# Layer 0's modulation steps ordered on TensorE behind the block traced before them

## The chip, the cores and the metric

The kernel runs on one core of one Trainium2 chip. The metric is the time of one execution in device microseconds (us), from the runtime's measurement; a profiled execution also leaves a trace, whose span runs from the first to the last instruction. Lower is better. Differences below about 0.2% are not told apart from none.

## The reference, cut to what matters

Two transformer-like layers are applied to 128 context tokens and 256 latent tokens (384 rows of 1024 features). Layer 0 mixes with two groups of linear recurrences (HGRN2 and gated DeltaNet), layer 1 with attention; each layer ends with an MLP. Every sub-layer is modulated by vectors that come from a conditioning vector and one matrix, `ada_w`, of 1024 x 6144 per layer:

```python
def _modulation(cond, w, b):
    m = jax.nn.silu(cond) @ w + b
    return jnp.split(m[:, None, :], 6, axis=-1)
...
        p_sh1, p_sc1, p_g1, p_sh2, p_sc2, p_g2 = _modulation(c_ctx[None, :], ada_w[l], ada_b[l])
        s_sh1, s_sc1, s_g1, s_sh2, s_sc2, s_g2 = _modulation(c, ada_w[l], ada_b[l])
        hp = _rmsnorm(xp, norm_g[l, 0]) * (1.0 + p_sc1) + p_sh1
...
        q_a, f_fw, f_bw, i_a, g_a, qkv_b, g_b, a_fw, a_bw, b_fw, b_bw = _split(h @ w_in, _AB_SIZES)
...
        xp = xp + p_g1 * mp
        hp = _rmsnorm(xp, norm_g[l, 1]) * (1.0 + p_sc2) + p_sh2
```

What the change moves is the part of layer 0's modulation that the mixer does not need at its start: the gate of the mixer (`g1`, columns 2048 to 3071 of `ada_w`), and the shift and scale of the MLP's norm (`sh2`, `sc2`, columns 3072 to 5119).

## The kernel before, in words

Everything is computed in float32 precision by pairs of reduced-precision products: each weight tile is loaded by the SP queue into a ring `raw`, split into a high part by ACT (L209) and a low part by DVE or POOL (L210), and multiplied on PE in three products (high by high, high by low, low by high).

The framework builds the queue of each engine ahead of time: it plays the program through a model of the chip and, whenever an engine is free, gives it the ready instruction that was traced earliest. The order thus made is fixed; on the chip each engine works through its own queue in that order, and waits where data are late. A context `issue_after` adds order edges to that planning: what is traced inside it on the engine of a given instruction is put in that engine's queue behind that instruction. It adds no instruction and no semaphore. The table `ORDER` (L40 to L49) and the method `behind` (L141) apply it: `self.mark` remembers an instruction under a name, and a block traced under a key of `ORDER` is queued behind the marks listed there.

Layer 0 is the function `layer0` (L1411). After a first part that ends with `gdn_solve` being traced (a triangular solve of 31 steps on POOL, L1052 and L1053), a hand-written list `STEPS` (L55) interleaves three generators with the blocks of the input projection:

- `h`, the HGRN2 chain (`hgrn_steps`, `hgrn_rest`): elementwise work on DVE (L746 to L783) between small products on PE (L745, L757, L762, L831 to L848);
- `d`, the DeltaNet chain (`gdn_steps`): products at L1086 to L1192;
- `a`, the modulation (`ada_rest`, L372);
- blocks `f`, `q`, `c` and `g` by `fm_block` (L633), each of 48 products at L645 to L647, and blocks `v` by `tm_half` (L677), each of 72 products at L687 to L689. In the list they stand in the order f3, f1, f2, q1, q0, c4, c5, v0, v1, c0, c1, g0, g1, g2, g3.

The modulation has twelve loading steps. Eight come from `ada_quad` (L313; here called S0 to S7): each loads two tiles of 512 KB (L323) and makes four products into one PSUM bank (L326), which the trace holds as eight records. Four come from `ada_half` (L353; H0 to H3), with loads at L362 and products at L367. All loads go through a ring `adr` of two slots, and one step fills both: the loads of a step can only start when the products of the step before have freed the slots. After S7 and after H3 the sums are copied to SBUF by DVE (L383 and L384, or L394), spread to columns by four small products into a bank called `tmp` (L488), and added to the bias (L490).

In `STEPS` the twelve steps are traced like this: S0 and S1 after q1; S2 and S3 after q0; S4 after q0 as well, ahead of c4; S5 after c4; S6 and S7 with the first spread after c5; H0 after v1; H1, H2, H3 with the second spread at the very end, after g3. The planner is free to queue them elsewhere.

Behind the list come `mix_out(1, t)` (L1255, through the same `tmp` bank), the output projection (`tm_parts`, products at L672 to L674), the residual and the norm of the MLP, which needs the result of H3, and the MLP.

Of the kernel before, what the change touches and what calls it, by code (L numbers as in the profile page):

```python
# [19 lines left out]
KT = 8  # L20
# [28 lines left out]
}  # L49

PARTS = [range(0, 2), range(2, 4), range(4, 6), range(6, 8)]
# [55 lines left out]
class Trunk:  # L107
# [525 lines left out]
    def fm_block(self, src, hh, evac, key):  # L633

        nc = self.nc
        hhi, hlo = hh
        raw = self.slab(src.rearrange("(k p) n -> p k n", p=P), KT, 256)
        whi, wlo = self.split_w(raw, KT, 256, pool=ON_POOL.get(key, ()))
        pg = [self.ps([P, T], "acc") for _ in range(2)]
        for g in range(2):  # L640
            with self.behind(key, g):
                for n in range(2):
                    c = slice(n * P, (n + 1) * P)
                    for k in range(g * 4, g * 4 + 4):
                        nc.tensor.matmul(pg[n], whi(k)[:, c], hhi[:, k], start=(k == 0), stop=False)  # L645
                        nc.tensor.matmul(pg[n], whi(k)[:, c], hlo[:, k], start=False, stop=False)  # L646
                        nc.tensor.matmul(pg[n], wlo(k)[:, c], hhi[:, k], start=False, stop=(k == KT - 1))  # L647
        for n in range(2):
            evac(n, pg[n])

# [26 lines left out]
    def tm_half(self, src, hh, evac):  # L677

        nc = self.nc
        hhi, hlo = hh  # L680
        whi, wlo = self.split_w(self.slab(src.rearrange("(k p) n -> p k n", p=P), KT, 256), KT, 256)
        for t0, n in ((0, 2), (2, 1)):
            pg = self.ps([P, 2, 256], "acc")[:, 0:n]
            for t in range(t0, t0 + n):
                c = slice(t * P, (t + 1) * P)
                for k in range(KT):
                    nc.tensor.matmul(pg[:, t - t0], hhi[:, k, c], whi(k), start=(k == 0), stop=False)  # L687
                    nc.tensor.matmul(pg[:, t - t0], hlo[:, k, c], whi(k), start=False, stop=False)
                    nc.tensor.matmul(pg[:, t - t0], hhi[:, k, c], wlo(k), start=False, stop=(k == KT - 1))  # L689
            evac(t0, n, pg)  # L690
            yield

# [718 lines left out]
    def layer0(self):  # L1411
        nc, i = self.nc, self.i
# [47 lines left out]
        def gate(b):  # L1460
            o = (2048, 2304, 4096, 4352)[b]
            self.fm_block(W[:, o:o + 256], hh, lambda n, pg: self.evac_gate(b * 2 + n)(pg), f"gate{b}")

        def value(b):
            for _ in self.tm_half(W[:, 1536 + b * 256:1792 + b * 256], hh, lambda t, n, pg: nc.scalar.activation(
                    self.va[:, t:t + n, b * 256:b * 256 + 256], pg, AF.Copy)):
                pass

        def hgrn():
            yield from self.hgrn_steps()  # L1470
            yield from self.hgrn_rest()

        chains = {"h": hgrn(), "d": self.gdn_steps(), "a": self.ada_steps}
        for step in STEPS.split():
            kind, n = step[0], int(step[1:] or 1)
            if kind in chains:
                for _ in range(n):
                    next(chains[kind], None)
            elif kind == "f":
                self.fm_block(fcol(n // 2, n % 2), hh, fgate(n // 2, n % 2), step)  # L1480
            elif kind == "q":
                self.fm_block(W[:, n * 256:n * 256 + 256], hh, lambda k, pg: self.evac_q(n * 2 + k)(pg), step)
            elif kind == "c":
                self.fm_block(qkv(n), hh, conv(n), step)
            elif kind == "v":
                value(n)
            elif kind == "g":
                gate(n)
            elif kind == "m":
                y = [self.sb([P, 4, T], "hyB", F32R) for _ in range(3)] + [self.m12([P, 4, T], F32R)]  # L1490
                yy = Halves(y[0::2]), Halves(y[1::2])
                for t in range(NT):
                    self.mix_out(0, t, yy, "hg")
# [6 lines left out]
        step = self.proj_residual(i["w_out_ab"][0], yy, scr, (("wo", "wo"), ("wo", "m12")), order,  # L1500
                                  lambda t: self.mix_out(1, t, yy, "tmp"))
# [10 lines left out]
        step = self.mlp(0, hh, order=order)  # L1512
# [308 lines left out]
```

## Time and profile before

| | |
|---|---|
| median of 3 runs | 1133.59 us (1132.84 to 1134.93) |
| the profiled execution | 1139.19 us |
| its span | 1137.3 us |
| PE busy | 1081.7 us |
| DVE busy | 762.3 us |
| POOL busy | 277.2 us |

Times in views count from the start of the span. A row of the timeline has the start, the length, the engine, the line, the operation, the tile written and those read, the shape and the count of merged instructions; idle time of the engine ahead of it stands in brackets with what ended it. Rows of DMA-issuing instructions (SPq) give the time of the issue, not of the transfer. In a table of windows each engine has its busy time and its number of instructions, then follow the granted clock of PE (1.00 is full), the busy share of the DMA engines and their rate.

### The profile page before, as it was taken

What the parts mean: (1) busy time and instruction counts of PE and PEld (TensorE: products, weight loads), DVE (VectorE), ACT (ScalarE), POOL (GpSimd) and SP (SyncE); (2) the same over time, 40 slices, a digit from 0 to 9 for tenths busy, and PEclk for the clock granted to TensorE, in tenths of its full rate; (3) what the DMA queues carried; (4) which work ended last, traced back from release to release, by engine and by line L of the source; (5) the groups of instructions that cost most, each with busy time, mean ns of one, the idle gap of its engine ahead of it and who ended that gap; (6) DMA issues with size and microseconds to landing.
All of it is one profiled execution on the core that took longest, in us unless ns stands there. A gap on an engine that the chain in (4) does not pass through costs nothing.

```text
span 1137.3 us, 17975 instructions
## 1 busy us (share of the span) xinstructions
PE 1081.7 (95%) x6853; PEld 937.8 (82%) x6853; DVE 762.3 (67%) x1188; ACT 485.1 (43%) x874; POOL 277.2 (24%) x295
## 2 busy tenths in 40 slices
PE   6989969999998999999999999999988999999998
PEld 3868857988986898888889788888668889998987
DVE  3678499995467698968887654878748773333333
ACT  4464333342445543433334444656636433333330
POOL 0054894231204011111112252324012011111102
PEclk9989989999998999999999999999989999999999
DMA  8953725333162687766674147566425764433301
GB/s 290 292 168 107 220 79 162 129 108 110 38 218 78 244 275 261 260 202 222 226 248 134 41 101 211 153 185 167 119 74 184 281 203 130 133 126 126 99 38 56
DMA packets 142091, 184.66 MB, mean 162 GB/s; under 512 B 36803, under 2 KB 113685, under 8 KB 142005
## 3 DMA queue, kind: packets, MB, share of 16 engines
q1 hardware_dynamic: 141685, 183.44, 51.0%
q8 instruction: 54, 0.88, 0.3%
q14 instruction: 32, 0.26, 0.1%
q10 hardware_dynamic: 320, 0.07, 0.0%
HBM read 171.53 MB, written 4.61 MB: 155 GB/s over the span
## 4 chain that ended last, share of the span: by engine, by line
PE 74%; DVE 7%; DMA 6%; POOL 6%; issue 2%; SPq 2%; ACT 2%; POOLq 0%; DVEq 0%; ACTq 0%
PE acc L1340 7%; PE acc L1341 7%; PE acc L1342 7%; PE tmp L1355 7%; PE tmp L1356 7%; PE tmp L1354 7%; POOL sm L1053 2%; POOL sm L1052 2%; PE po L1731 2%; DMA ada<-in_ada_w 2%; PE acc L646 2%; PE acc L645 2%; PE acc L647 1%; PE acc L672 1%; PE acc L673 1%
## 5 line engine op out<-in xcount | busy, mean ns | idle before, releaser
L210 DVE TENSOR_TENSOR wlo<-raw,whi 128x1024 fp32r<-128x1024 f32 x192 | 238.0, 1250 | 167.2 <-ACT whi L209 145.5
L209 ACT ACTIVATE whi<-raw 128x1024 fp32r<-128x1024 f32 x198 | 205.9, 1050 | 335.0 <-PE acc L1342 190.6
L1374 POOL TENSOR_TENSOR h<-h 128x384 f32<-128x384 f32 x56 | 69.5, 1242 | 424.9 <-ACT h L1371 423.7
L1341 PE MATMUL acc<-wlo,h 128*128 128x512 f32 x380 | 148.5, 391 | 0.1
L1340 PE MATMUL acc<-whi,h 128*128 128x512 f32 x380 | 146.0, 393 | 0.6 <-issue 0.6
L346 DVE SCALAR_TENSOR_TENSOR adc<-adr,scz,adc 128x1024 f32<-128x1024 f32 x98 | 128.5, 1342 | 10.3 <-DMA adr<-in_ada_w 10.1
L1342 PE MATMUL acc<-whi,h 128*128 128x512 f32 x380 | 121.2, 391 | 0.0
L1340 PEld LDWEIGHTS acc<-whi,h 128*128 128x128 f32 x380 | 71.2, 188 | 20.6 <-ACT whi L209 5.0
L1355 PE MATMUL tmp<-hyA,whi 128*128 128x384 f32 (+1 forms) x256 | 85.1, 333 | 2.2 <-DVE hyA L565 2.2
L1354 PE MATMUL tmp<-hyA,whi 128*128 128x384 f32 (+1 forms) x256 | 84.1, 334 | 3.0 <-DVE hyA L564 3.0
L1354 PE MATMUL tmp<-hyB,whi 128*128 128x384 f32 (+1 forms) x256 | 83.8, 329 | 1.2 <-DVE hyB L564 1.2
L1356 PE MATMUL tmp<-hyA,wlo 128*128 128x384 f32 (+1 forms) x256 | 84.8, 332 | 0.0
L1355 PE MATMUL tmp<-hyB,whi 128*128 128x384 f32 (+1 forms) x256 | 84.0, 329 | 0.7 <-DVE hyB L565 0.7
L1341 PEld LDWEIGHTS acc<-wlo,h 128*128 128x128 f32 x380 | 71.4, 188 | 14.3 <-DVE wlo L210 0.5
L1342 PEld LDWEIGHTS acc<-whi,h 128*128 128x128 f32 x380 | 71.0, 188 | 13.7
L1356 PE MATMUL tmp<-hyB,wlo 128*128 128x384 f32 (+1 forms) x256 | 82.1, 328 | 0.0
L645 PE MATMUL acc<-hyA,whi 128*128 128x384 f32 x208 | 74.1, 356 | 0.0
L646 PE MATMUL acc<-hyA,whi 128*128 128x384 f32 x208 | 71.4, 343 | 0.0
L647 PE MATMUL acc<-hyA,wlo 128*128 128x384 f32 x208 | 71.0, 342 | 0.0
L1375 DVE TENSOR_TENSOR h<-h,h 128x384 fp32r<-128x384 f32 (+2 forms) x72 | 37.8, 526 | 40.6 <-POOL h L1374 39.8
L1354 PEld LDWEIGHTS tmp<-hyA,whi 128*128 128x128 f32 x256 | 48.7, 191 | 4.4 <-ACT km L560 3.4
L1355 PEld LDWEIGHTS tmp<-hyA,whi 128*128 128x128 f32 x256 | 49.3, 192 | 3.3 <-DVE hyA L565 2.4
(454 smaller groups left out, 2357.7 us busy)
## 6 DMA issues: line engine op xcount, KB each, us to landing
raw<-in_w_mlp SPq DMA_DIRECT2D x128, 512.0 KB, 3.8
adr<-in_ada_w SPq DMA_DIRECT2D x80, 512.0 KB, 4.7
raw<-in_w_in_ab SPq DMA_DIRECT2D x34, 512.0 KB, 4.7
ada<-in_ada_w SPq DMA_DIRECT2D x32, 256.0 KB, 5.5
raw<-in_w_qkv_na SPq DMA_DIRECT2D x32, 256.0 KB, 3.8
raw<-in_w_out_ab SPq DMA_DIRECT2D x8, 512.0 KB, 4.5
m<-gs SPq DMA_DIRECT2D x8, 512.0 KB
raw<-in_w_qkv_na SPq DMA_DIRECT2D x8, 512.0 KB
```

Of the source, the lines that this page charges most:

```text
L209: self.nc.scalar.activation(hi, x, AF.Copy)
L210: (eng or self.nc.vector).tensor_tensor(lo, x, hi.bitcast(F32), op=ALU.subtract)
L346: nc.vector.scalar_tensor_tensor(acc[v], raw, s[v], acc[v], op0=ALU.mult, op1=ALU.add)
L645: nc.tensor.matmul(pg[n], whi(k)[:, c], hhi[:, k], start=(k == 0), stop=False)
L646: nc.tensor.matmul(pg[n], whi(k)[:, c], hlo[:, k], start=False, stop=False)
L647: nc.tensor.matmul(pg[n], wlo(k)[:, c], hhi[:, k], start=False, stop=(k == KT - 1))
L1340: nc.tensor.matmul(pg, shi, w2hi(n)[:, o], start=start, stop=False)
L1341: nc.tensor.matmul(pg, shi, w2lo(n)[:, o], start=False, stop=False)
L1342: nc.tensor.matmul(pg, slo, w2hi(n)[:, o], start=False, stop=last)
L1354: nc.tensor.matmul(pg[n], w1hi(k)[:, c], hhi[:, k, tc_], start=(k == 0), stop=False)
L1355: nc.tensor.matmul(pg[n], w1hi(k)[:, c], hlo[:, k, tc_], start=False, stop=False)
L1356: nc.tensor.matmul(pg[n], w1lo(k)[:, c], hhi[:, k, tc_], start=False, stop=(k == KT - 1))
```

## The change

The last product of each call of `fm_block` and `tm_half` is remembered under the mark "block", and each step of the modulation in the list is traced under the key ("step", "a"), which `ORDER` now ties to that mark. So the products of a step (L326, L367, and the spread's L488, which is traced in the same call as S7 or H3) are queued on PE behind the last product of the latest block traced ahead of it. The keys of the other two generators are not in `ORDER`; for them the context does nothing.

```diff
     ("last", 0, 2, 1): [("T", 0, 0), ("T", 0, 1)],
     ("w1", 0): [("D", 0), ("A", 0)],
+    ("step", "a"): ["block"],
 }
...
-                        nc.tensor.matmul(pg[n], wlo(k)[:, c], hhi[:, k], start=False, stop=(k == KT - 1))
+                        self.mark["block"] = nc.tensor.matmul(pg[n], wlo(k)[:, c], hhi[:, k], start=False, stop=(k == KT - 1))
...
-                    nc.tensor.matmul(pg[:, t - t0], hhi[:, k, c], wlo(k), start=False, stop=(k == KT - 1))
+                    self.mark["block"] = nc.tensor.matmul(pg[:, t - t0], hhi[:, k, c], wlo(k), start=False, stop=(k == KT - 1))
...
             if kind in chains:
                 for _ in range(n):
-                    next(chains[kind], None)
+                    with self.behind("step", kind):
+                        next(chains[kind], None)
```

## The prediction

> **What bounds the kernel now.** I read the page first, then windows over the stretch in which the change acts, then the timelines of PE, DVE and SP at the places of the moved steps.
>
> ```profile
> span 1137.3 us, 17975 instructions
> PE 1081.7 (95%) x6853; PEld 937.8 (82%) x6853; DVE 762.3 (67%) x1188; ACT 485.1 (43%) x874; POOL 277.2 (24%) x295
> ...
> PE 74%; DVE 7%; DMA 6%; POOL 6%; issue 2%; SPq 2%; ACT 2%; POOLq 0%; DVEq 0%; ACTq 0%
> ```
>
> PE is busy 95% of the span and holds 74% of the chain that ended last. An average hides stages, so windows come next; the columns are the window, its length, then PE, PEld, DVE, ACT and POOL busy (with counts), the granted clock and the DMA share.
>
> ```profile
> 80.00:85.00 5.00, 4.38 (x15) 2.19 (x13) 1.32 (x3) 4.85 (x7) 2.78 (x4) 0.50 0.40 132
> 85.00:90.00 5.00, 5.00 (x22) 3.91 (x21) 3.64 (x8) 3.68 (x12) 2.31 (x3) 0.77 0.31 105
> 61.80:119.30 57.50, 54.45 (x274) 42.37 (x273) 44.38 (x74) 31.65 (x64) 25.73 (x27) 0.91 0.45 138
> 119.30:142.00 22.70, 21.76 (x175) 17.93 (x175) 12.16 (x12) 7.68 (x11) 21.25 (x27) 1.00 0.64 220
> 142.00:181.00 39.00, 27.34 (x352) 21.96 (x351) 38.97 (x48) 11.80 (x21) 36.18 (x41) 0.89 0.32 109
> 181.00:323.00 142.00, 139.39 (x1475) 129.23 (x1475) 104.59 (x192) 55.42 (x129) 33.18 (x39) 0.99 0.36 109
> 323.00:349.30 26.30, 26.30 (x124) 21.60 (x123) 16.30 (x26) 10.39 (x23) 4.32 (x4) 1.00 0.53 170
> ```
>
> In three stages PE is full: 119 to 142 (21.76 of 22.70), 181 to 323 (139.39 of 142.00) and 323 to 349 (all). Between 142 and 181 it is not: it idles 39.00 - 27.34 = 11.66 us, while DVE is busy 38.97 of 39.00. So up to 142 PE's queue sets the pace, then DVE, then PE again until the projection is done at 349. Behind that the change moves nothing. The end is therefore PE's work up to 349, which the change does not alter, plus its idle time up to there; what the change is worth is what it does to that idle time.
>
> **The steps as they lie.** Twelve steps, S0 to S7 and H0 to H3; the rows below are S1's second half, S2, S3, S4 (two halves), S6, H1, H2 (two halves) and H3, with the block products next to some of them.
>
> ```profile
> 83.28 1.92 PE L326 MATMUL ada<-adr,scz 128*32 128x512 f32 x4
> ...
> 100.16 1.06 PE L326 MATMUL ada<-adr,scz 128*32 128x512 f32 x8
> 101.15 0.45 PE L645 MATMUL acc<-hyA,whi 128*128 128x384 f32 x1
> ...
> 109.70 1.07 PE L326 MATMUL ada<-adr,scz 128*32 128x512 f32 x8
> 110.70 0.44 PE L645 MATMUL acc<-hyA,whi 128*128 128x384 f32 x1
> ...
> 118.95 0.34 PE L647 MATMUL acc<-hyA,wlo 128*128 128x384 f32 x1
> 119.96 1.05 PE L326 MATMUL ada<-adr,scz 128*32 128x512 f32 x4 [0.67 <-DMA adr<-in_ada_w]
> 121.29 1.05 PE L326 MATMUL ada<-adr,scz 128*32 128x512 f32 x4 [0.28 <-DMA adr<-in_ada_w]
> 122.28 0.44 PE L645 MATMUL acc<-hyA,whi 128*128 128x384 f32 x1
> ...
> 164.88 1.09 PE L326 MATMUL ada<-adr,scz 128*32 128x512 f32 x8
> ...
> 249.97 1.07 PE L367 MATMUL ada<-adr,scz 128*32 128x512 f32 x8
> ...
> 255.16 1.05 PE L367 MATMUL ada<-adr,scz 128*32 128x512 f32 x4 [1.20 <-DMA adr<-in_ada_w]
> ...
> 256.73 1.05 PE L367 MATMUL ada<-adr,scz 128*32 128x512 f32 x4
> ...
> 275.14 1.06 PE L367 MATMUL ada<-adr,scz 128*32 128x512 f32 x8
> ...
> 319.38 0.34 PE L647 MATMUL acc<-hyA,wlo 128*128 128x384 f32 x1
> ```
>
> A step costs PE 1.0 us (100.16 to the next product at 101.15). The row at 118.95 is q1's last product, the one at 319.38 is g3's. The edges thus move S0 to S5 (S0 and S1 to behind q1; S2, S3 and S4 to behind q0; S5 to behind c4) and H1 to H3 (from 250 to 276, to behind 319). S6 at 164.88, S7 and H0 are queued behind their blocks already: nothing changes for them. Their SP loads and DVE copies have no edge, and POOL has no part in them; but a step fills both slots of the ring, so each load waits for the products of the step before, and moves along. The edges themselves add no instruction and no wait.
>
> **Front, S0 to S5.** Taken out ahead of q0's first product at 122.28: S2 0.99, S3 1.00, and from q1's end (118.95 + 0.34) to 122.28 another 2.99 for S4 with its waits. S1's second half at 83.28 lies in the chain before products that DVE needs; it took 1.92, but DVE idled only this long for what came of it:
>
> ```profile
> 88.16 0.17 DVE L961 TENSOR_SCALAR ksq<-ksq 128x12 f32<-128x12 f32 x1 [0.69 <-ACT cv L954]
> ```
>
> so its removal is worth 0.69, at most 1.92; I take 0.69. S0 and S1's first half lie where PE goes idle right after: nothing. Put back ahead of q0's end: S0 and S1, 2.0, and a wait of S1 for its load, which now can only be asked for when S0's products are done. How long is a load, and what does PE lose to it?
>
> ```profile
> DMA to landing us min/median/max: 4.1/4.4/4.7
> ```
>
> The planner fills such a gap with other products, by its own idea of a load; what PE lost in spite of that is in the two steps above that ran right behind their loads, S4 (0.67 + 0.28 = 0.95) and H2 (1.20). The bounds are 0 (S2, S3 and S6 show no wait) and a whole load, 4.4; I take 1.1 a step, by the steps that are most alike. So q0 ends 0.69 + 0.99 + 1.00 + 2.99 - 2.0 - 1.1 = 2.6 us earlier, and with it starts the HGRN2 chain that keeps DVE full. c4, however, comes behind q0 and gets S2, S3 and S4 beside it: 3.0 of work and 3.3 of waits, less S5's 1.0 that leaves it, so its end comes 6.3 - 1.0 - 2.6 = 2.7 later, and DVE's queue, fixed in order, holds the convolutions of c4 between parts of the HGRN2 chain. The front is worth between -2.6 (DVE's earlier start counts) and +2.7 (c4's lateness counts). PE's 11.66 us of idle time just behind are the cover for the second; I take 0, the middle.
>
> **Tail, H1 to H3.** Their 3 us of work and the second spread leave a full stage and enter a full stage: 0. H2's wait of 1.20 goes. New: H1 runs behind g3, H2's load follows H1, H3's follows H2. Two waits, each between 0 (the projection's products cover it) and 4.4; I take H2's own 1.2, together +2.4. Their loads pass to another stretch of SP's queue, which is served in order:
>
> ```profile
> 314.23 0.37 SPq L204 DMA_DIRECT2D raw<-in_w_out_ab  x1
> 315.30 0.34 SPq L512 DMA_DIRECT2D m<-gs  x1
> 315.95 0.38 SPq L1224 DMA_DIRECT2D out_state_gdn<-sm  x1
> 316.39 0.49 SPq L512 DMA_DIRECT2D m<-gs  x1
> 322.12 0.37 SPq L204 DMA_DIRECT2D raw<-in_w_out_ab  x1
> ...
> 330.22 0.37 SPq L204 DMA_DIRECT2D raw<-in_w_out_ab  x1
> ```
>
> ```profile
> SPq L204 <- DVE wlo L210: 14.2, 2, 9.1
> ...
> SPq L204 <- DVE wo L210: 4.8, 2, 4.1
> ```
>
> From 316.88 to 322.12 SP waits for DVE to free a weight slot: 5.2 us. A load of H2 or H3 queued behind such a wait is late by up to that, two by 5.2 + 4.1 = 9.3; one queued ahead of it makes weights wait for PE instead. Bounds 0 to 9.3; I take a quarter of 5.2, 1.3, since the loads at L362 were held so in none of the nearest cases around 250 to 258. The copy (DVE, 0.69 in the row of L384 below) goes into a stage where DVE is busy 16.30 of 26.30: covered; if not, 0.7.
>
> The spread uses the bank `tmp`, which the first transposes of `mix_out(1, t)` use next. That the turn goes by the order of tracing is seen at the first spread: its data were ready at 182.1, but it ran at 216.78, behind transposes of c5 that were traced earlier.
>
> ```profile
> 181.40 0.69 DVE L384 COPY ada<-ada 64x512 f32<-64x512 f32 x1
> ...
> 212.62 0.55 PE L949 MATMUL tmp<-ident,cv 128*128 128x128 f32 x3
> ...
> 216.78 0.83 PE L488 MATMUL tmp<-ident,ada 128*128 128x4 f32 x6
> ```
>
> So the transposes of the tile that comes first there wait for H3's spread: from g3's end 1.0 + 2 x (0.8 for two issues, by the rows of SP above, + 4.4 + 1.0) + 0.7 + 0.8 = 15 us. Meanwhile PE has the 72 products of the projection that do not need them, at 26.30 / 124 = 0.21 each: 15 us. Just covered: 0; each us by which the spread is later than that costs one. The norm, which needs H3's result, starts after the projection's end at 349 and is not reached: g3's end at 319.7 plus 15 is 335.
>
> **Sum**: 0 - 1.2 + 2.4 + 1.3 = +2.5 us. The profiled execution took 1139.19, 1.9 over its span and 5.6 over the median; it would become 1141.7, and the median 1133.59 + 2.5 = 1136.1.
>
> **A rule that speaks against the change.** S1's second half took 1.92 us where the same records take 1.05 at 119.96: in the window 80 to 85 the granted clock is 0.50, in 85 to 90 it is 0.77. [...] The trace agrees that the clock falls where PE waits and returns after it is busy. S0 and S1 are filler just there: without them the window 85 to 90 could stay at 0.50, which costs (0.77 - 0.50) x 5 = 1.35 us of f1's products.
>
> **Rivals.**
> - *The front counts* (ends on the other side). DVE is the bound from 142 on and its chain starts 2.6 us earlier; c4's lateness falls into PE's idle time; the tail's loads are not held and its two waits are covered like the transposes. Then -2.6 - 1.2 = -3.8: 1129.8. It decides by whether the first HGRN2 instruction of DVE (L746) starts over 2 us earlier and c4's convolutions do not hold it up. For it: DVE's 38.97 of 39. Against: five steps in a row behind their loads.
> - *A load is caught behind SP's wait for weights.* One row shows what that is like, of SP's waits between 84 and 103, ahead of S3's loads:
>
> ```profile
> SPq L204 <- DVE wlo L210: 16.3, 1, 16.3
> ```
>
>   That was 16.3 us; it did no harm because nothing was queued tightly behind S3. Now it would: PE would stand. With one wait of 5.2 beyond the forecast: +7.7, 1141.3.
> - *PE's idle time absorbs all* (the edges are kept, but cost and gain nothing): the waits of S1 to S5 fall into the 11.66 us, those of H2 and H3 into the projection: 0, 1133.6.
> - *The clock stays low longer*, by the mechanism above: 2.5 + 1.35 = +3.9, 1137.5.
>
> **How the numbers follow.** A measurement of this kernel tells about 0.2% (2.3 us) from no change. Forecast (waits behind loads cost 1 to 5 us): chance 0.33, of which 0.21 slower and 0.12 within. The front counts: 0.29, 0.27 of it faster and 0.02 within. Caught load: 0.16, slower. All absorbed: 0.15, 0.13 within, 0.01 to each side. Clock: 0.07, 0.06 slower, 0.01 within. Together faster 0.28, same 0.28, slower 0.44. The likeliest time is 1136.1, its own range 1134.6 to 1138.6 (1 to 5 us). The range over all takes in the front's rival with 0.8 us to spare (1129.0) and the caught load with 1.7 to spare (1143.0); two catches in the tail (9.3) and a front worth more than 2.6 lie outside.
>
> **What would show each step.** Right: no record of L326 between 62 and q1's end, S0 directly behind it; PE rows of L326 and L367 with idle time until a DMA on adr at S1 to S5, H2 and H3, about 1 us each; L367 at three places behind g3; L488 of H3 and then L1262 on `tmp` behind them; the projection's end later by 2 to 3 us. Wrong, to the fast side: idle of PE in the stage after 142 shrinks by over 2 us and L746 comes first over 2 us earlier, with no idle rows at L367. Wrong, to the slow side: one idle row at L326 or L367 of over 4 us. The clock's rival shows as a window at 0.50 beyond 88.

## The result, and the profile after

The changed kernel takes 1149.49 us (median of 4 runs, 1146.75 to 1150.98) against 1134.26 (4 runs, 1132.84 to 1136.66) of the kernel before on the same chip: a ratio of 1.0129, 95% interval 1.0101 to 1.0157, some 15 us slower. 1136.1 was forecast, with a range up to 1143.0. Of the experiments below, one execution of before (5955.63 us) and the profiled one of e11 (5384.34 us) took some five times as long as all others; they are left out, so e11 has no trace to compare. In the kernel after, line numbers behind L47 are one higher (L327 is L326 of before).

The page of the profiled execution (1150.98 us):

```profile
span 1149.1 us, 18000 instructions
...
PE 1088.6 (95%) x6853; PEld 938.8 (82%) x6853; DVE 761.1 (66%) x1188; ACT 485.6 (42%) x874; POOL 273.5 (24%) x295
...
PE 76%; DVE 7%; POOL 7%; DMA 4%; issue 2%; SPq 2%; ACT 1%; DVEq 0%; POOLq 0%; ACTq 0%
```

The same 6853 products keep PE busy for 6.9 us more, and PE waits 4.9 us more. The groups of PE, first of before, then of after, show most of the extra work in the steps:

```profile
L326 PE MATMUL ada<-adr,scz 128*32 128x512 f32 x64 | 15.5, 661 | 1.0 <-DMA adr<-in_ada_w 0.9
...
L367 PE MATMUL ada<-adr,scz 128*32 128x512 f32 x32 | 5.3, 604 | 1.2 <-DMA adr<-in_ada_w 1.2
```

```profile
L327 PE MATMUL ada<-adr,scz 128*32 128x512 f32 x64 | 20.4, 723 | 6.7 <-DMA adr<-in_ada_w 6.7
...
L368 PE MATMUL ada<-adr,scz 128*32 128x512 f32 x32 | 6.3, 605 | 1.1 <-DMA adr<-in_ada_w 1.1
```

The timeline of PE helps to see why the steps themselves became dearer by 5.9 us (20.4 + 6.3 - 15.5 - 5.3), and where the two longest waits for their loads are:

```profile
115.66 1.06 PE L327 MATMUL ada<-adr,scz 128*32 128x512 f32 x8
...
125.65 1.05 PE L327 MATMUL ada<-adr,scz 128*32 128x512 f32 x4
...
127.90 1.05 PE L327 MATMUL ada<-adr,scz 128*32 128x512 f32 x4
...
148.36 1.07 PE L327 MATMUL ada<-adr,scz 128*32 128x512 f32 x2 [6.16 <-DMA adr<-in_ada_w]
...
323.87 1.06 PE L368 MATMUL ada<-adr,scz 128*32 128x512 f32 x8
...
330.05 1.05 PE L368 MATMUL ada<-adr,scz 128*32 128x512 f32 x4 [1.13 <-DMA adr<-in_ada_w]
...
334.23 1.05 PE L368 MATMUL ada<-adr,scz 128*32 128x512 f32 x4
...
339.76 1.05 PE L368 MATMUL ada<-adr,scz 128*32 128x512 f32 x4
...
343.26 1.05 PE L368 MATMUL ada<-adr,scz 128*32 128x512 f32 x4
...
348.71 0.95 PE L489 MATMUL tmp<-selc,ada 128*128 128x4 f32 x8
349.93 0.66 PE L1263 MATMUL tmp<-ident,hyB 128*128 128x128 f32 x4 [0.27 <-DVE A L491]
351.38 0.65 PE L1263 MATMUL tmp<-ident,hyB 128*128 128x128 f32 x4 [0.79 <-DVE g L1265]
...
364.79 1.03 PE L554 MATMUL tmp<-ident,xh 128*128 128x128 f32 x8
```

S0 stands behind q1's last product, as the edge wants. The four products of a step write four strips of 32 partitions of one bank and run side by side (a record takes 0.6 us and more, eight of them together 1.06); the two products of a half take 1.05 as well. So a step that runs in two halves, each behind the load of its own tile, costs PE twice as much. In before six of the twelve steps ran so (S0, S1, S4, S5, S7 and H2), in after nine do (S1 to S7, H2 and H3). That makes some 3 of the 5.9 us; S3 and S4 besides ran at a low granted clock (0.50 from 148 to 152, 0.62 from 160 to 164). The next step's first load can start when the first half has freed its slot, its second load only behind the second half (SP issues H3's two at 331.14 and 335.33, right behind H2's halves). The chain H1, H2, H3, spread takes 25.8 us from g3's end to the spread's end (323.9 to 349.66), not 15. Waiting for loads is only a part of that, for PE has other products all the while: H3's tiles have landed at 335.2 and 338.9 by the trace, its halves run at 339.76 and 343.26 behind products of the projection that stand ahead of them in PE's queue, and the spread runs 3.3 us behind the end of its copy on DVE. The transposes of `mix_out` on `tmp` come right behind it, at 349.93 and 351.38 (the last two of three, 326.29 and 330.50 in before; the first, at 333.70, is queued ahead of the spread), and the first transposes of the norm at 364.79 instead of 349.34. The wait of 6.16 us at S3 is the load caught behind weights that one rival spoke of, though in the front; SP's waits from 120 to 150:

```profile
SPq L205 <- POOL wlo L211: 12.5, 1, 12.5
```

Four windows, the stretches from 62.8 to q1's end, to c5's end, to g3's end, and to the first transposes of the norm; then one for the clock:

```profile
62.80:115.70 52.90, 45.66 (x244) 41.18 (x244) 43.56 (x72) 28.42 (x61) 23.60 (x22) 0.90 0.23 68
115.70:172.00 56.30, 45.81 (x424) 32.16 (x425) 41.81 (x44) 18.26 (x30) 49.72 (x58) 0.91 0.58 185
172.00:323.90 151.90, 145.91 (x1554) 133.35 (x1554) 113.07 (x202) 56.90 (x132) 40.51 (x53) 0.99 0.33 103
323.90:364.80 40.90, 38.71 (x186) 27.79 (x186) 19.74 (x32) 12.63 (x28) 5.33 (x5) 0.96 0.55 181
...
350.00:355.00 5.00, 4.21 (x15) 3.12 (x16) 3.87 (x7) 1.86 (x3) 0.00 (x0) 0.71 0.23 57
```

The same three stretches behind q1 in before:

```profile
119.30:164.70 45.40, 36.85 (x397) 31.22 (x401) 34.82 (x38) 15.28 (x25) 42.58 (x48) 0.92 0.43 145
164.70:319.70 155.00, 148.33 (x1583) 134.61 (x1584) 118.59 (x210) 57.53 (x133) 47.02 (x59) 0.99 0.36 112
319.70:349.30 29.60, 29.60 (x153) 24.88 (x151) 18.61 (x29) 12.50 (x28) 5.33 (x5) 1.00 0.53 175
```

q1 ends 3.6 us earlier (115.7, was 119.3). From there to c5's end it takes 56.30 instead of 45.40, with 9.0 us more of PE's work. From c5 to g3's end it takes 3.1 less, with H1 to H3 gone from it. From g3 to the norm it takes 40.9 instead of 29.6. The norm starts at 364.79, 15.5 us later than in before and 13.7 later than in a second trace of before (e8 below), and from there to the end after takes 784.3 us, between these two (788.0 and 782.2): the whole loss lies ahead of the norm.

### The profile page after: what moved, and what is told of

Its sections match the earlier page's. It is cut to its first block, busy times and chain, and to the rows that moved or that the text cites. A ratio compares the mean times of both kernels' runs of the same rounds, so it can differ in the third digit from the quotient of the medians.

```text
span 1149.1 us, 18000 instructions
## 1 busy us (share of the span) xinstructions
PE 1088.6 (95%) x6853; PEld 938.8 (82%) x6853; DVE 761.1 (66%) x1188; ACT 485.6 (42%) x874; POOL 273.5 (24%) x295
## 4 chain that ended last, share of the span: by engine, by line
PE 76%; DVE 7%; POOL 7%; DMA 4%; issue 2%; SPq 2%; ACT 1%; DVEq 0%; POOLq 0%; ACTq 0%
PE tmp L1356 8%; PE tmp L1357 7%; PE tmp L1355 7%; PE acc L1341 7%; PE acc L1342 7%; PE acc L1343 7%; POOL sm L1054 2%; POOL sm L1053 2%; PE acc L673 2%; PE po L1733 2%; PE acc L674 2%; PE acc L646 2%; PE acc L675 2%; PE acc L647 2%; PE acc L648 1%
## 5 line engine op out<-in xcount | busy, mean ns | idle before, releaser
L1375 POOL TENSOR_TENSOR h<-h 128x384 f32<-128x384 f32 x56 | 65.2, 1165 | 427.8 <-ACT h L1372 426.2
L1343 PEld LDWEIGHTS acc<-whi,h 128*128 128x128 f32 x380 | 71.0, 188 | 13.7
```

The source lines that it names most:

```text
L1343: nc.tensor.matmul(pg, slo, w2hi(n)[:, o], start=False, stop=last)
```

## The experiments

Every kernel was timed beside the kernel before on the same chip; e8 was only profiled. A ratio has its 95% interval; "us" is the ratio less 1, times the median of before in that group. "g0 to norm" is read from each trace: from the end of g0's last product to the start of the norm's first transposes, the stretch in which H1 to H3 move. It depends on the front too, since the edges there change how much of the two chains lies ahead of g0; so it is compared only between kernels whose front is tied alike: before, e1, e6 to e10, e13 and e14 on the one hand, after, e2 and e5 on the other.

| run | edit | ratio | us | g0 to norm |
|---|---|---|---|---|
| before | - | 1 | 0 | 99.3 |
| after | the change | 1.0129 (1.0101 to 1.0157) | +14.6 | 108.6 |
| e1 | only H1 to H3 tied | 1.0105 (1.0076 to 1.0133) | +11.9 | 108.1 |
| e2 | only S0 to S7, H0 tied | 1.0032 (1.0015 to 1.0048) | +3.6 | 99.2 |
| e3 | only S0, S1 tied | 1.0039 (1.0023 to 1.0055) | +4.4 | 99.6 |
| e4 | only S2 to S4 tied | 1.0011 (0.9993 to 1.0028) | +1.3 | 104.2 |
| e5 | the change, spread on `ada` | 1.0094 (1.0065 to 1.0124) | +10.7 | 104.5 |
| e6 | e1, spread on `ada` | 1.0065 (1.0042 to 1.0088) | +7.4 | 104.6 |
| e7 | e1, H1 to H3 behind g2 | 1.0045 (1.0025 to 1.0065) | +5.1 | 106.7 |
| e8 | before, profiled again | - | - | 99.3 |
| e9 | before without H1 to H3 | 1.0060 (1.0038 to 1.0082) | +6.8 | 100.1 |
| e10 | e6, `mix_out` traced first | 1.0053 (1.0034 to 1.0072) | +6.0 | 104.6 |
| e11 | before, `mix_out` traced first | 1.0014 (0.9998 to 1.0030) | +1.6 | - |
| e12 | only S2 to S7, H0 tied | 1.0002 (0.9982 to 1.0023) | +0.2 | 107.9 |
| e13 | before, H1 to H3 without loads | 0.9993 (0.9980 to 1.0007) | -0.8 | 98.8 |
| e14 | e6 with dummy products | 1.0082 (1.0064 to 1.0100) | +9.3 | 108.9 |
| e15 | e3, S0 and S1 without loads | 1.0073 (1.0055 to 1.0090) | +8.3 | 105.9 |
| e16 | e3 without S2 and S3 | 1.0100 (1.0072 to 1.0128) | +11.4 | 102.1 |
| e17 | before without S0 and S1 | 1.0022 (1.0008 to 1.0036) | +2.5 | 101.0 |

Behind the norm no edit adds or leaves out an instruction, but the planner's order there is not always that of before. Read by line from the traces of PE, DVE, ACT and POOL, e2, e3, e4 and e12 keep the order of before to the end; after, e6, e10, e13, e14 and e15 share a second order of layer 1; e1, e5, e9, e16 and e17 share a third; e7 has its own. From the norm to the end the traces take 781.3 to 790.2 us, and those of before alone 782.2 to 788.0. The second order costs nothing that can be seen (e13, -0.8); what the third costs is not known, for no kernel has it and is otherwise like before.

The first theory (A) was that about 9 us are lost in the front and 6 in the tail; its rivals put everything in one of the two.

### e1 to e4: which edges

The edges are switched by the index of the step (0 to 7 are S0 to S7, 8 is H0, 9 to 11 are H1 to H3); TIED is range(9, 12), range(0, 9), range(0, 2) and range(2, 5).

```diff
-        chains = {"h": hgrn(), "d": self.gdn_steps(), "a": self.ada_steps}
+        chains = {"h": hgrn(), "d": self.gdn_steps(), "a": self.ada_steps}; nth = iter(range(12))
...
-                    with self.behind("step", kind):
+                    with self.behind("step", kind if kind != "a" or next(nth) in TIED else "free"):
```

> Only H1, H2, H3 and the second spread are tied to the block ahead of them (g3); S0 to S7 and H0 are free. Two places theory (A): the loss of 15 us is made in the front (about 9) and in the tail (about 6: from g3's end to the first transposes of the norm it went from 29.6 to 40.9 us, +11.2, less the 4.9 of work and wait that H1 to H3 took ahead of g3 before). Then this one is 5 to 7 us slower than before. Tail theory (B): what is lost in the front falls into idle time and comes back by the time g3 ends, the turn of the bank tmp behind the spread makes all of it: then 12 to 15 slower. Front theory (C): the tail only moves work: 0 to 2 slower.

> S0 to S7 and H0 are tied to the block ahead of them; H1 to H3 and the second spread are free. By (A) g3 ends about 9 us later than before and all of it reaches the end: 8 to 10 slower. By (B) 0 to 2 slower. By (C) 12 to 15 slower.

> Only S0 and S1 are tied (behind q1); all other steps are free. In after, q1 ended 3.6 us earlier and q0 0.6 earlier. If the steps behind q1 are harmless (A), this one is between 2 faster and 2 slower. If the work that leaves the first blocks is what makes PE idle there (PE's idle time between 62 us and q1's end rose from 3.0 to 7.2) and that counts (D), it is 4 slower by itself.

> Only S2, S3 and S4 are tied (behind q0); all others are free. In after, S3 waited 6.16 us for a load that stood in SP's queue behind a wait for a weight slot, and c4 ended 9.1 later. By (A), with the caught load in this place, 6 to 9 slower. If the front's loss is S0's and S1's doing (D), 0 to 2.

The tail costs 11.9 us, the front 3.6, together 15.5: within the intervals the two parts add up to the whole, but the other way round than (A) had it. (In the traces the norm comes 6.0 to 7.7 us late in e1 and 3.0 to 4.8 in e2, against 13.7 to 15.5 in after, so the good sum is in part luck.) Within the front S0 and S1 are enough for all of it (e3). S2 to S4 alone cost 1.3, which can't be told from nothing, although there too a step stands behind its caught load, for longer than in after:

```profile
145.07 1.92 PE L327 MATMUL ada<-adr,scz 128*32 128x512 f32 x4 [8.43 <-DMA adr<-in_ada_w]
```

So the caught load, the most conspicuous row of the trace, is not by itself what the front pays for.

In the stretch from g0 to the norm, tying H1 to H3 costs 8.8 us with a free front (108.1 for 99.3) and 9.4 with a tied one (108.6 in after for 99.2 in e2). The median says 11.9; the six executions of e1 scatter from 1143.6 to 1155.2, the longer ones at a lower mean clock (0.974 for the longest, 0.984 for the shortest), and the one with the profile is the shortest; a part of its 11.9 may also come from the third order behind the norm. The tail of e1, from the timeline of PE:

```profile
341.45 1.06 PE L489 MATMUL tmp<-selc,ada 128*128 128x4 f32 x8 [0.79 <-DVE ada L395]
342.78 0.66 PE L1263 MATMUL tmp<-ident,hyB 128*128 128x128 f32 x4 [0.27 <-DVE A L491]
344.22 1.12 PE L1263 MATMUL tmp<-ident,hyB 128*128 128x128 f32 x4 [0.79 <-DVE g L1265]
```

The order is as in after: H3, spread, then the transposes on `tmp`, with short waits between, for each hands on to the next. The windows, from g3's end to the norm, and of those waits:

```profile
320.80:357.10 36.30, 34.46 (x154) 24.13 (x154) 16.57 (x25) 9.96 (x16) 4.67 (x4) 0.95 0.52 175
342.00:346.00 4.00, 2.95 (x16) 2.43 (x16) 2.78 (x6) 1.23 (x2) 0.00 (x0) 0.69 0.00 0
```

### e5 to e8: the bank, and one block sooner

Theory T: the turn of `tmp` makes the tail's loss; rival W: the moved work does. e5 is the change, e6 is e1, each with H3's spread on the bank `ada`; e7 is e1 with another place in the list.

```diff
-        self.ada_spread(A, rows, self.sel, "p q (n v) -> p v n q", self.ada_bias(0, 4))
+        self.ada_spread(A, rows, self.sel, "p q (n v) -> p v n q", self.ada_bias(0, 4), "ada")
...
-    def ada_spread(self, out, rows, pick, order, bias):
+    def ada_spread(self, out, rows, pick, order, bias, tag="tmp"):
...
-        pt = self.ps([P, 4, 4], "tmp")
+        pt = self.ps([P, 4, 4], tag)
```

```diff
-c0 h3 c1 h5 d2 h d2 h d h7 g0 g1 d m g2 g3 a3
+c0 h3 c1 h5 d2 h d2 h d h7 g0 g1 d m g2 a3 g3
```

> The whole change, but H3's spread takes the bank ada instead of tmp, so that the transposes of mix_out need not wait for it. Theory T (the turn of tmp makes the tail's loss): the tail's 12 us shrink to the moved work, 0 to 3, and with the front's 3.6 this is 3 to 7 us slower than before instead of 15. Rival W (the tail's loss is the moved work itself, three split steps behind their loads on SP's queue): 11 to 15 slower, as in after.

> Only H1, H2, H3 and the second spread are tied (behind g3), and the spread takes the bank ada. T: the transposes L1263 on tmp come within 12 us of g3's end and the first transposes of the norm within 32 of it (29.6 before, 36 in the same kernel with the spread on tmp); 0 to 3 slower than before. W: norm at 34 to 37 behind g3, 8 to 12 slower.

> Only H1, H2, H3 and the second spread are tied, and they are traced one block earlier, behind g2 instead of g3; the spread stays on tmp. T: the spread comes about 21 us after g2's end, at 320 to 327, and the transposes on tmp wait 0 to 4 us for it instead of 15: 0 to 4 slower. W: the same steps with the same split and the same waits for loads, only one block sooner: 8 to 12 slower.

> The kernel before, unchanged, profiled once more: which milestones differ between two executions of one program. If the profile of before is typical, q1's end, g3's end and the first transposes of the norm (119.3, 319.7, 349.3) come again within 1 us; if they move by 3 or more, differences of that size between other traces mean nothing.

The bank is worth 3.9 us in the whole change (10.7 for 14.6) and 4.5 in the tail alone (7.4 for 11.9); the traces have 4.1 and 3.5 for it (104.5 for 108.6, 104.6 for 108.1). In time alone the intervals of each pair overlap; it is the four figures together that put it at about 4. So T is right for about a third of the tail and W for the rest; neither got its number. e6 on PE, without the waits, and its windows from g0's end to g3's end and on to the norm:

```profile
342.69 0.88 PE L1263 MATMUL tmp<-ident,hyB 128*128 128x128 f32 x6
...
344.42 1.05 PE L368 MATMUL ada<-adr,scz 128*32 128x512 f32 x4
...
350.60 0.95 PE L489 MATMUL ada<-selc,ada 128*128 128x4 f32 x8
```

```profile
252.00:324.20 72.20, 67.25 (x496) 65.37 (x494) 41.77 (x81) 28.75 (x89) 12.03 (x12) 0.98 0.23 73
324.20:356.60 32.40, 32.40 (x150) 22.55 (x150) 16.34 (x25) 9.88 (x16) 4.34 (x4) 1.00 0.59 196
```

The spread now comes behind the transposes, nothing is late behind it, PE is busy throughout and its clock full (0.95 in e1). This stretch is 2.8 us longer than in before (32.40 for 29.60). The stretch ahead of it, which the steps have left, is longer too (72.20 for 69.70 in before): 32 records that run behind g3 in before (products of the DeltaNet chain and transposes on `hg`) are now queued ahead of it, and PE's idle time there is 4.95 us, where e8 has 2.55. e7 gets rid of the wait in another way (its spread runs at 331.86, its transposes at 336.85) and loses 5.1. e8 puts q1, g3 and the norm at 118.3, 321.5 and 351.1, against 119.3, 319.7 and 349.3: two executions of one program differ by up to 1.8 us at a milestone, but "g0 to norm" agrees to 0.1. As far as two executions can tell, differences of 1 us in this stretch therefore mean something, those of single milestones only above 2 us.

### e9 to e12: what the steps did where they stood

Theory F: in their old place H1 to H3 were filler. e9 leaves them out of before:

```diff
         for r in range(4):
+            if r:
+                yield
+                continue
...
-                    nc.tensor.matmul(pm[32 * j:32 * j + 32], self.sc[:, 2 * kt:2 * kt + 32], w[g][:, n], start=(r == 0), stop=(r == 3))
-            if r < 3:
-                yield
+                    nc.tensor.matmul(pm[32 * j:32 * j + 32], self.sc[:, 2 * kt:2 * kt + 32], w[g][:, n], start=True, stop=True)
```

e10 is e6, e11 is before, with this; e12 has TIED = range(2, 9):

```diff
         if late:
+            for t in order:
+                late(t)
             for k in range(2):
...
-                if k == 0:
-                    for t in order:
-                        late(t)
```

> The kernel before, with the loads and products of H1, H2 and H3 left out (the scale of the MLP's norm is then built from H0 alone); the spread stays. What are these steps worth where they stood, between 250 and 276? Theory F (they were filler: they stood in waits of PE for the two chains, and without them PE waits there, 1.7 us in the tail-only kernel): 0 to 2.5 faster than before. The prediction's picture (work in a full stage): their 4.2 of work and H2's wait of 1.2 go, 4.5 to 6 faster.

> As e6 (H1 to H3 and the second spread behind g3, the spread on the bank ada), and the three mix_out(1, t) are traced ahead of the projection's products instead of behind the first 48. Theory O (with PE later and the weights there, the planner takes the 48 products that are traced first, and the transposes come 15 us later than they could): the first transposes of the norm come 29 to 31 us behind g3's end instead of 32.4, and the time is 2 to 5 slower than before instead of 7.4. If the rest of the loss is the moved steps' work and the lost filler (F), the order makes no difference: 6 to 9 slower.

> The control of e10: the kernel before, with the three mix_out(1, t) traced ahead of the projection's products and nothing else. In before the transposes already slip in between the products at 319, 326 and 330: within 1.5 us of before by O and by F.

> S2 to S7 and H0 are tied to the block ahead of them; S0, S1 and H1 to H3 are free. Theory R (the ring of two slots: S0, freed at 70 in before and at 114 after, holds all later steps back, and so S2 to S5 run beside c4 and c5 up to 190): without that 0 to 2 slower. Rival (S2 to S5 beside c4 are what costs, whenever S0 runs): 3 to 5 slower, as with S0 to S7 tied (3.6).

e9 is the surprise: without the steps the kernel is not faster, by little or by much, but 6.8 us slower. In the trace their stretch doesn't shrink (g0 to norm 100.1, was 99.3). The timeline of PE in e9 has waits just behind the old place of the steps (its last row is the start of the norm), and the windows are g0's end to g3's end and the end of these waits:

```profile
280.48 1.13 PE L1179 MATMUL gd<-sm,m 128*128 128x128 f32 x8 [0.58 <-DVE m L1011]
...
283.34 2.04 PE L1179 MATMUL gd<-sm,m 128*128 128x128 f32 x8 [1.73 <-DVE m L1011]
...
286.62 3.60 PE L1179 MATMUL gd<-sm,m 128*128 128x128 f32 x16 [1.23 <-ACT g L1185]
...
350.83 1.03 PE L554 MATMUL tmp<-ident,xh 128*128 128x128 f32 x8
```

```profile
250.70:321.20 70.50, 64.64 (x462) 63.07 (x462) 37.91 (x76) 24.95 (x77) 10.20 (x10) 0.95 0.20 62
...
285.00:290.00 5.00, 3.77 (x18) 3.47 (x17) 1.13 (x4) 2.42 (x9) 0.00 (x0) 0.51 0.00 0
```

In e8, the kernel before, the same stretch reads:

```profile
251.90:321.50 69.60, 67.05 (x490) 61.96 (x489) 38.24 (x76) 26.19 (x78) 10.59 (x10) 1.00 0.29 92
```

PE has 28 records less, but it idles 5.86 us instead of 2.55, for DVE and ACT, and its clock falls to 0.51 behind these waits, so that what is left takes longer (eight records of L1179 1.13 us at 280.48, 2.04 at 283.34). So the work that filled this stage was not what bound it: 4.2 us of products and a wait of 1.2 are gone, and the stretch up to the norm is 0.8 longer. The 6.8 us are not made there, though. In e9 the norm starts at 350.83, against 349.34 and 351.12 in the two traces of before, and behind it e9 takes 790.2 us against 788.0 and 782.2 (its profiled execution, 1142.83 us, is the median one). So the loss lies behind the norm, where the work is that of before and the queues have the third order; whether that order makes it isn't shown. What e9 says of the steps is its stretch, not its time.

e10 with its control e11 shows nothing clear: 6.0 for 7.4, with intervals that overlap. Theory O is not borne out (g0 to norm stays at 104.6). e12 shows that tying S2 to S7 costs nothing clear (+0.2) as long as S0 and S1 are free.

### e13 to e15: products or loads

```diff
             for g in range(2):
+                if r:
+                    w = keep
+                    continue
                 w.append(self.sb([P, 2, 512], self.ada_ring))
...
+            keep = w
             for g in range(2):
                 kt = 4 * g + r
```

That is e13. e14 adds to e6 what stands first below, called ahead of the list's last entry and tied to g0's last product; e15 changes e3 as below it.

```diff
+    def fill(self):
+        pm = self.ps([P, 512], "tmp")
+        with self.behind("fill", 0):
+            for kt in range(12):
+                for q in range(4):
+                    j = kt % 4
+                    self.nc.tensor.matmul(pm[32 * j:32 * j + 32, q * P:(q + 1) * P], self.sc[:, 2 * j:2 * j + 32], self.c["ident"],
+                                          start=True, stop=True)
```

```diff
-            w = []
+            w = [self.x[:, 0, 0:512]] * 4 if kt < 2 else []
             for j in range(0, 4, 2):
+                if kt < 2:
+                    continue
                 raw = self.sb([P, 2, 512], self.ada_ring)
```

> The kernel before, with the six loads of H1, H2 and H3 left out; their products stay and read the tiles of H0 (so the scale of the MLP's norm is another). Theory F (the products are filler of PE's waits behind g0): within 2.5 us of before, to either side, although the same kernel without the products was 6.8 slower. Rival L (it is the loads that matter, or the order of SP's queue): 5 to 8 slower, as without both.

> As e6 (H1 to H3 and the second spread behind g3, the spread on the bank ada), plus three steps' worth of dummy products (48 of 128x128, results read by nothing), queued behind g0's last product and traced behind g3. F: the waits of PE behind g0 fall from 1.7 to under 0.8 us, and the kernel is 0.5 to 4 slower than before in spite of some 5 us of useless products. Rival (PE's waits there are not the cause): the products are added to e6's 7.4: 8 to 13 slower.

> As e3 (S0 and S1 tied behind q1, all else free), but the four loads of S0 and S1 are left out and their products read a resident tile (so the mixer's gate and the norm's shift are other numbers). The place of the products is that of e3, and the ring's two slots are free for S2 from the start. Theory R (the ring holds S2 to S7 back): within 2 us of before. Rival P (the products behind q1 are what costs, or their absence ahead of it): 3 to 6 slower, as e3 (4.4).

e13: with the products in place and the loads gone the time is that of before. So the loads of H1 to H3 are free. How much the products count is not shown by the 6.8 us of e9, which lie behind the norm, where the two kernels differ in order; in the stretch they are 1.3 us apart (98.8 and 100.1). e14 goes against F all the same. The dummies do fill the gap behind g0, as the timeline of PE shows:

```profile
251.48 0.84 PE L380 MATMUL tmp<-ident,scz 128*32 128x128 f32 x6
...
252.84 1.53 PE L380 MATMUL tmp<-ident,scz 128*32 128x128 f32 x18
```

and no wait is left in it. But the kernel is at +9.3, not back at 0.5 to 4. Up to g3's end e14 takes 72.4 us, as e6 does (72.2), in spite of the dummies; from there to the norm it takes 36.5 instead of 32.4, for the 32 records that e6 has ahead of g3 are behind it again. So the dummies took the place of other work, which went behind g3: filling PE's waits is not by itself what H1 to H3 did. e15 takes the loads away as the cause of S0's and S1's cost: without them the kernel is 8.3 slower, more than either side expected. It does not set S2 to S7 free, for all eight steps add into one bank in turn (L326), and S2 still runs behind S0 and S1, at 129.25; but e12 has S2 to S7 late too, and costs nothing.

### e16 and e17: why S0 and S1

```diff
         for kt in range(KT):
+            if kt in (2, 3):
+                yield
+                continue
```

e17 has `kt < 2` in this place in the kernel before, with `start=(kt == 2)`.

> As e3 (S0 and S1 tied behind q1, all else free), but S2 and S3 are left out, loads and products (the mixer's gate and the norm's shift lack a quarter of their sum). Theory Q (the stretch from q1's end to c5's end, in which PE is not full, takes some steps for nothing but not six: before has two there, e12 four, e3 six): four are left there, c5 ends 45 to 50 us behind q1 (57 in e3), and the kernel is between 2 faster and 1.5 slower than before. Rival P (moving S0 and S1 costs by itself): 3 to 6 slower, as e3 (4.4).

> The kernel before, with S0 and S1 left out, loads and products; S2 to S7 are free. Q: nothing is added behind q1, two steps' work is gone: between 2.5 faster and 0.5 slower. Rival P2 (their absence ahead of q1 is what costs, as leaving out H1 to H3 cost 6.8): 3 to 7 slower.

Q falls: with two steps less in that stretch the kernel is slower than e3, not faster, and c5 ends 54.8 us behind q1 (170.9 and 116.1). e17 is at +2.5, between the two expectations, and its norm comes at 353.53, 2.4 to 4.2 us late. So part of the cost of S0 and S1 seems to be that they are missing ahead of q1; what the rest is, stays open. The three kernels that leave products out (e9, e16, e17) are slower than before by 2.5 to 11.4 us, e16 also than e3 with the same edges, and e13, which leaves out loads alone, is not. In e16 (norm at 359.50, in e3 at 355.90) and e17 the loss shows ahead of the norm, in e9 behind it. What is common to the three is that the planner orders all queues anew around the hole, and that they have the third order behind the norm. That an order is the cause was not shown: no kernel left the products out and kept the order of the rest.

No run was faster than the kernel before by more than its interval.

## Why the prediction was wrong

Its direction was right, its size was not: +2.5 forecast, some 15 measured. The right direction was mostly luck, for it came from waits that hardly show (see below), while the two terms that it put at 0, the front and the moved work, made most of the loss. By its own steps:

- **Front, "I take 0, the middle".** 3.6 us (e2). The edges did what was said (S0 directly behind q1, none of the steps ahead of it), and q1 ends 3.6 earlier. But q0 ends 0.6 earlier instead of 2.6, and c4 9.2 later (152.9, was 143.7) instead of 2.7. "A step costs PE 1.0 us" failed first: behind their loads most steps run in halves of 1.05 each, as S4 does in the prediction's own rows. The wait of 1.1 a step wasn't there; S3 waited 6.16 once, S7 0.53. Moving S2 to S7 cost nothing clear (e12, +0.2), so a cover of the kind that PE's 11.66 us of idle time were taken for was there; S0 and S1, costed at nothing where they leave, are the ones that cost (e3, +4.4; left out, e17, +2.5).
- **Tail, "Their 3 us of work and the second spread leave a full stage and enter a full stage: 0".** This step failed most: the tail costs 7.4 us without any turn of the bank (e6). The stage they enter is full, and there they take 6.2 us of PE (1.06 and four times 1.05, and 0.95 for the spread, by the rows of after). The stage they leave gives little or nothing back: from g0's end to g3's end after takes 67.7 us where e2 has 69.6, e6 72.2 where before has 69.7, and e9, without the steps at all, 70.5. Its work was not what bound it: PE waits there for the two chains instead. The two windows looked alike, 98 and 100% busy. Why e6 loses 7.4 where its trace has 5.3 of it (104.6 for 99.3) stays open.
- **"Just covered: 0; each us by which the spread is later than that costs one".** The mechanism was right for two of the three tiles: their transposes stand behind H3's spread. The chain was mis-sized: 25.8 us in after and 21.7 in e1 (320.8 to 342.51) instead of 15, because H2 and H3 run in halves with loads of their own and because PE's queue puts products of the projection ahead of halves whose tiles have landed. The cover was a little smaller: 60 products of the projection ran ahead of the spread, not 72. The price was not one for one: the bank is worth 3.9 and 4.5 us where 10.8 and 6.7 were late.
- **SP's queue, 1.3, and H2's and H3's waits, 2.4.** One wait of 1.13 is seen in the tail, and nothing caught there. The load caught (12.5 us on SP) was S3's, and e4 shows that such a load alone need not cost.
- **Norm not reached.** The result of H3 is there in time: in after the spread is done at 349.7, and the first transposes of the norm come at 364.8, late by the projection.
- **"Behind that the change moves nothing."** The order of layer 1's queues does change, but without a cost that shows (784.3 us from the norm to the end, in before 788.0 and 782.2).
- **Clock.** The clock does not fall at every wait of PE: in before it did at two of 1.17 (0.71 from 75 to 80), but not at H2's of 1.20 (1.00 from 250 to 283). The rival's 1.35 us was the author's estimate from two windows of before, and no run shows it. At the place that the rival named nothing happens: the windows of after, without S0 and S1, there read

```profile
80.00:85.00 5.00, 3.22 (x15) 3.23 (x16) 1.95 (x4) 4.86 (x13) 2.05 (x3) 0.50 0.27 93
85.00:90.00 5.00, 5.00 (x24) 4.04 (x24) 3.58 (x11) 4.82 (x12) 1.70 (x3) 0.91 0.00 0
```

  with 0.91 where before had 0.77. It falls in the tail instead, behind the waits around the spread: 0.71 from 350 to 355 is worth 1.5 us by an estimate (0.29 of 5).

The sum that the runs give: 3.6 for the front, about 4.5 for the bank, 7.4 for the moved steps, 15.5 in all, each to some 2 or 3 us. Why the front's part hangs on S0 and S1 stays open.

## What to carry to other kernels

An engine that is busy throughout a stage need not be bound by the work in it, above all where a scheduler has placed that work: before you book a gain for moving it away, ask what the engine would wait for without it, or leave the work out and read that stretch of the trace. The time of the whole kernel can mislead there: a scheduler may answer the hole with another order far behind it, as in e9. Work moved behind a barrier costs its time where that stage is full, and takes along its ring of buffers and the banks that later work uses in turn. When a trace has one conspicuous wait, make the kernel without it before you call it the cause.

## What the runs showed of the hardware

**DVE beside POOL.** A split of one tile (128x1024) on DVE took 1.23 us at 118.39 in after and 1.22 at 117.04 in e5; the next one in e5 took 5.59. The timeline of DVE in e5, then that of POOL:

```profile
120.97 5.59 DVE L211 TENSOR_TENSOR wlo<-raw,whi 128x1024 fp32r<-128x1024 f32 x1 [2.71 <-ACT whi L210]
```

```profile
121.08 1.26 POOL L740 TENSOR_TENSOR km<-x 128x512 f32<-128x512 f32 x1
122.30 0.37 POOL L1053 TENSOR_TENSOR sm<-sm,sm 96x112 f32<-96x112 f32 x1
122.63 1.26 POOL L740 TENSOR_TENSOR km<-x 128x512 f32<-128x512 f32 x1
123.85 0.41 POOL L1054 TENSOR_TENSOR sm<-sm,sm 96x112 f32<-96x112 f32 x1
124.22 1.26 POOL L740 TENSOR_TENSOR km<-x 128x512 f32<-128x512 f32 x1
125.44 1.44 POOL L1053 TENSOR_TENSOR sm<-sm,sm 96x135 f32<-96x135 f32 x1
126.95 0.46 POOL L1054 TENSOR_TENSOR sm<-sm,sm 96x135 f32<-96x135 f32 x1
```

DVE's instruction lasts while six of POOL's follow each other without a pause; the sixth, in which it ends, takes 1.44, the next one of the same shape 0.46. In after, whose queues of DVE and POOL are the same up to there, this split took 1.38, and it was an instruction of POOL that took longer (L1054 on 96x87, 1.22 instead of 0.36): which of the two takes longer, and by how much, differed between these two executions. What makes them longer is not shown. PE waits for L707, which DVE does next: 1.24 us in after, 7.35 in e3.

**The clock fell without a long wait.** In e1 no wait between 340 and 345 is longer than 0.79 us, and the granted clock still falls (0.69 in the window 342 to 346 above), with PE busy for 2.95 of 4.00; in after it is 0.71 behind waits of 0.27 and 0.79. Whether it was the short waits together or the kind of work is not shown, for between the waits PE had only transposes and the spread's products of four columns.
